# The first transfers of a two-layer encoder trunk, laid anew by k-tile

## The chip, the core and the metric

The kernel runs on one core of a Trainium2 chip. The time is device microseconds (us) of one execution on that core. A profiled execution leaves a page and a trace, from which all rows below are taken. Engines are named as the profile names them: PE multiplies matrices, PEld loads its stationary operands, DVE and ACT work elementwise, POOL does small scalar work, SP issues most transfers; q at the end of a name (SPq, ACTq) is the engine's instruction queue, where transfers are issued.

## The reference, cut to what matters

The input x has 256 tokens of 1024 columns. Two layers follow each other; each normalises, multiplies by one wide projection w_in, runs two attention branches, merges them, and goes through a gated feed-forward block and a per-layer embedding. Only the first instructions of the first layer are touched:

```python
u = rms_norm(h, g_mix_pre)                    # h = x, gain g of 1024 columns
(gq, gk, gv, gg, ra_f, ra_b, aq, ak, av, gate_a, gate_b) = jnp.split(u @ w_in, offsets, axis=-1)
```

The kernel multiplies first by 1056 columns of w_in, from column 3072 on: 32 of the two decay ranks (ra_f, ra_b) and 1024 of the attention's queries (aq). It cuts them in blocks of 288, 384 and 384 (`RQ`). The row factor of the norm is applied after the product, so that the product can start from x times the gain.

## The kernel before, in words

Every product is done in three passes to keep float32 precision: an operand is split in a high part (rounded to the matmul's format fp32r) and a low part, the rest; the passes are high by high, high by low, low by high. For weights ACT casts `wh` from the raw tile and DVE subtracts to get `wl`; for activations ACT makes `high` from the transposed x in PSUM times the gain, and DVE makes `rest` (`rest` is named `low` for weights).

Weights come in units of about 1 MB (`Stream`, lines 248 to 366), through two raw buffers. The first four units are rows 0 to 255, 256 to 511 and so on of those 1056 columns; a unit holds two k-tiles of 128 rows. `FIRST` (line 54) cuts the first unit's transfer into one for each k-tile. `load` (line 285) issues the next unit's transfer when a raw buffer is promised, and calls `between` after each piece.

The start is an order written out by hand. `on` (line 139) ties each instruction to the one before it on the same `line` (engine or transfers), so that their order is kept. `start()` (line 830) is a generator: it issues some work, yields a count of ticks, and goes on after so many calls of `tick()`, which the matmul loops make. Before: x's first 512 columns of tokens 0 to 127 go on SP and of tokens 128 to 255 on ACT, then the gain; then unit 0 in two pieces, unit 1 whole, and x's other columns. PE runs warm-up matmuls on constants (`WARM`: 6 of 128 columns, 6 of 512, and 3 more of 512 after the first transposes). `gains` turns the gain, `turn(hf, k)` transposes 128 columns of one token half, `high` and `rest` split the result.

`rq_first` (line 1034) multiplies unit 0 k-tile by k-tile for both token halves, six PSUM accumulators at once, 18 matmuls a k-tile; the units 1 to 3 go through `rq_step` (line 1026), one accumulator at a time. `STEPS_FIRST` gives the order of units. The third unit (unit 2) is split inside `start()` at its end, from unit 3 on by `fill`. The small weights of the decay (`up_weights`, line 730, six transfers at lines 737 and 738) are issued behind whatever stood last on the transfers' line when the layer loop begins (line 942). A scheduler then orders each engine's instructions by its own estimate of when they are ready, within those ties, for the whole program.

The transfers of a queue use eight completion semaphores in turn, so a ninth transfer waits until the first has landed.

## Time and profile before

| | us |
|---|---|
| median of 3 runs | 922.12 (921.61 to 922.44) |
| the profiled execution | 921.18 |
| its span, first to last instruction | 919.5 |
| PE busy in it | 909.8 |

The span leaves out 1.7 us of the execution's own time. The page lists busy time by engine, the span in 40 slices, the transfers, the chain of work that ended last and the costliest groups; the trace answers for a stretch (timeline, windows) or for one tile. In a timeline a row merges instructions of one kind: start, length from the first start to the last end, engine, line, operands, count, and in brackets the idle time before it and what ended it. Instructions that go through `on` all have line 142, `mm` has 105, `passes` has 121.

### The profile page before, as it was taken

What the parts mean: (1) busy time and instruction counts of PE and PEld (TensorE: products, weight loads), DVE (VectorE), ACT (ScalarE), POOL (GpSimd) and SP (SyncE); (2) the same over time, 40 slices, a digit from 0 to 9 for tenths busy, and PEclk for the clock granted to TensorE, in tenths of its full rate; (3) what the DMA queues carried; (4) which work ended last, traced back from release to release, by engine and by line L of the source; (5) the groups of instructions that cost most, each with busy time, mean ns of one, the idle gap of its engine ahead of it and who ended that gap; (6) DMA issues with size and microseconds to landing.
All of it is one profiled execution on the core that took longest, in us unless ns stands there. A gap on an engine that the chain in (4) does not pass through costs nothing.

```text
span 919.5 us, 12425 instructions
## 1 busy us (share of the span) xinstructions
PE 909.8 (99%) x4673; PEld 775.9 (84%) x4673; DVE 783.3 (85%) x1003; ACT 582.7 (63%) x970; POOL 91.7 (10%) x149
## 2 busy tenths in 40 slices
PE   9999999999999999999999999999999999999996
PEld 8998888888888888888899988888888788888885
DVE  7889989987669998999779789798875899989984
ACT  7678767564567565566676687765544766565663
POOL 4700221300100000000114002200001000000000
PEclk9999999999999999999999999999999999999999
DMA  8663445657395655657576424454673846555361
GB/s 291 205 189 133 138 138 189 212 184 244 109 301 186 210 191 201 228 166 262 190 232 220 148 92 140 136 208 159 211 247 110 279 160 211 222 175 216 138 229 46
DMA packets 88679, 173.44 MB, mean 189 GB/s; under 512 B 3422, under 2 KB 26470, under 8 KB 88108
## 3 DMA queue, kind: packets, MB, share of 16 engines
q1 hardware_dynamic: 88460, 172.40, 55.5%
q8 instruction: 36, 0.59, 0.3%
q10 hardware_dynamic: 160, 0.27, 0.1%
q14 instruction: 23, 0.19, 0.1%
HBM read 169.50 MB, written 3.15 MB: 188 GB/s over the span
## 4 chain that ended last, share of the span: by engine, by line
PE 91%; DVE 3%; ACT 2%; DMA 2%; issue 1%; POOL 1%; ACTq 0%; POOLq 0%; DVEq 0%; SPq 0%
PE acc_0ffnin L121 12%; PE acc_1ffnin L121 11%; PE acc_0gate L121 7%; PE acc_1gate L121 7%; PE acc_0ffnin L105 7%; PE acc_1ffnin L105 7%; PE acc_0gqk L121 2%; PE acc_0wout L121 2%; PE acc_1gqk L121 2%; PE acc_1ple L121 2%; PE acc_1gg L121 2%; PE acc_0v L121 2%; PE acc_0merge L121 2%; PE acc_1merge L121 2%; PE acc_0gg L121 2%; PE acc_0rq L121 2%
## 5 line engine op out<-in xcount | busy, mean ns | idle before, releaser
L105 PE MATMUL acc_0ffnin<-wh_0ffnin,big_0ffnin 128*128 128x512 f32 x176 | 57.0, 393 | 0.0
L105 PE MATMUL acc_1ffnin<-wh_1ffnin,big_1ffnin 128*128 128x512 f32 x176 | 56.8, 392 | 0.0
L133 ACT CAST wh_1ffnin<-raw_1ffnin 128x1024 fp32r<-128x1024 f32 x38 | 38.5, 1048 | 26.0 <-PE acc_1ffnin L121 7.8
L133 ACT CAST wh_0ffnin<-raw_0ffnin 128x1024 fp32r<-128x1024 f32 x38 | 38.3, 1048 | 24.9 <-DMA raw_0ffnin<-in_w_ffn_out_dram 7.6
L133 DVE TENSOR_TENSOR wl_1ffnin<-raw_1ffnin,wh_1ffnin 128x1024 fp32r<-128x1024 f32 x38 | 44.9, 1221 | 7.9 <-ACT wh_1ffnin L133 7.8
L133 DVE TENSOR_TENSOR wl_0ffnin<-raw_0ffnin,wh_0ffnin 128x1024 fp32r<-128x1024 f32 x38 | 44.7, 1221 | 7.8 <-ACT wh_0ffnin L133 7.8
L121 PE MATMUL acc_1ffnin<-wh_1ffnin,big_1wout 128*128 128x512 f32 x168 | 42.5, 393 | 0.0
L121 PE MATMUL acc_0ffnin<-wh_0ffnin,big_0wout 128*128 128x512 f32 x168 | 42.4, 393 | 0.0
L105 PEld LDWEIGHTS acc_0ffnin<-wh_0ffnin,big_0ffnin 128*128 128x128 f32 x176 | 33.0, 188 | 7.1 <-DVE big_0ffnin L133 0.4
L105 PEld LDWEIGHTS acc_1ffnin<-wh_1ffnin,big_1ffnin 128*128 128x128 f32 x176 | 33.0, 188 | 6.7
L133 DVE TENSOR_TENSOR wl_1ffnin<-lent_1ffnin,wh_1ffnin 128x1024 fp32r<-128x1024 f32 x30 | 35.8, 1219 | 1.8 <-ACT wh_1ffnin L133 1.8
L133 DVE TENSOR_TENSOR wl_0ffnin<-lent_0ffnin,wh_0ffnin 128x1024 fp32r<-128x1024 f32 x30 | 35.8, 1219 | 1.7 <-ACT wh_0ffnin L133 1.7
L121 PEld LDWEIGHTS acc_1ffnin<-wh_1ffnin,big_1wout 128*128 128x128 f32 x168 | 31.1, 188 | 6.2
L121 PEld LDWEIGHTS acc_0ffnin<-wh_0ffnin,big_0wout 128*128 128x128 f32 x168 | 31.1, 188 | 6.2
L133 ACT CAST wh_1ffnin<-lent_1ffnin 128x1024 fp32r<-128x1024 f32 x30 | 30.7, 1053 | 7.9 <-PE acc_1ffnin L105 3.9
L133 ACT CAST wh_0ffnin<-lent_0ffnin 128x1024 fp32r<-128x1024 f32 x30 | 30.7, 1053 | 6.9 <-PE acc_0ffnin L105 3.9
L105 PE MATMUL acc_0ffnin<-wl_0ffnin,big_0ffnin 128*128 128x512 f32 x88 | 34.3, 390 | 0.0
L105 PE MATMUL acc_1ffnin<-wl_1ffnin,big_1ffnin 128*128 128x512 f32 x88 | 34.3, 389 | 0.0
L133 DVE TENSOR_TENSOR wl_0gate<-raw_0gate,wh_0gate 128x1024 fp32r<-128x1024 f32 x20 | 24.0, 1247 | 6.8 <-ACT wh_0gate L133 6.7
L133 ACT CAST wh_0gate<-raw_0gate 128x1024 fp32r<-128x1024 f32 x20 | 20.0, 1049 | 13.9 <-DMA raw_0gate<-in_w_o_attn_dram 6.1
L133 DVE TENSOR_TENSOR wl_1gate<-raw_1gate,wh_1gate 128x1024 fp32r<-128x1024 f32 x20 | 23.6, 1220 | 5.4 <-ACT wh_1gate L133 5.4
L133 ACT CAST wh_1gate<-raw_1gate 128x1024 fp32r<-128x1024 f32 x20 | 20.0, 1051 | 11.6 <-DMA raw_1gate<-in_w_o_attn_dram 5.6
(705 smaller groups left out, 2701.9 us busy)
## 6 DMA issues: line engine op xcount, KB each, us to landing
raw_0ffnin<-in_w_ffn_out_dram SPq DMA_DIRECT2D x11, 1024.0 KB, 6.0
raw_1ffnin<-in_w_ffn_out_dram SPq DMA_DIRECT2D x11, 1024.0 KB, 5.6
lent_0ffnin<-in_w_ffn_in_dram SPq DMA_DIRECT2D x6, 1024.0 KB, 7.6
lent_1ffnin<-in_w_ffn_in_dram SPq DMA_DIRECT2D x6, 1024.0 KB, 7.1
raw_0v<-in_w_in_dram SPq DMA_DIRECT2D x4, 1024.0 KB, 5.0
raw_0gate<-in_w_o_gla_dram SPq DMA_DIRECT2D x4, 1024.0 KB, 5.1
raw_0gate<-in_w_o_attn_dram SPq DMA_DIRECT2D x4, 1024.0 KB, 5.2
raw_0wout<-in_w_ffn_in_dram SPq DMA_DIRECT2D x8, 512.0 KB, 6.4
```

The costliest lines, as they stand in the source:

```text
L105: return nc.tensor.matmul(o, lhsT, rhs, start=start, stop=stop)
L121: nc.tensor.matmul(o, x, y, start=start and n == 0, stop=stop and n == len(seq) - 1, **kw)
L133: return nc.scalar.copy(hi, src), nc.vector.tensor_tensor(out=lo, in0=src, in1=hi.bitcast(F32), op=ALU.subtract)
```

## The change

x is loaded in four transfers of all 256 tokens: columns 0 to 127 first, then 128 to 255, 256 to 511 and 512 to 1023, all on SP; the gain is the first transfer on ACT's queue. Of the weights the first transfer is 288 columns of k-tile 0, then its other 768, x's next columns, k-tile 1, x's next, k-tiles 2 and 3 apart, x's last. The warm-up on PE is 6 + 3 + 1 matmuls in place of 6 + 6 + 3. The first `high` of token half 1 is made by DVE. Unit 1 is also multiplied by `rq_first`, and transposes and splits are spread over the ticks of both units, so the transfers of `up_weights` are now tied behind x's last columns, and no longer behind the load of unit 2.

```diff
--- before.py
+++ after.py
@@ -49,9 +49,9 @@
 UNIT = 2112
 RQ = ((0, 288), (288, 672), (672, 1056))
 
-WARM = 6, 6, 3
-
-FIRST = (0, 0, 1056), (1, 0, 1056)
+WARM = 6, 3, 1
+
+FIRST = ((0, 0, 288), (0, 288, 1056), (1, 0, 1056)), ((0, 0, 1056), (1, 0, 1056))
 C_GQ, C_GK, C_GV, C_GG, C_RA = 0, 512, 1024, 2048, 3072
 C_AQ, C_AK, C_GA, C_GB = 3104, 4128, 4640, 5664
 
@@ -149,12 +149,10 @@
 
     grow = mid()[0:8, 0:P]
 
-    def load_x(hf, j, e="dma", q=nc.sync):
-        c = slice(j * 512, (j + 1) * 512)
-        on(e, q.dma_start, h[:, hf, c], a["x"][0, hf * P : (hf + 1) * P, c])
-
-    load_x(0, 0)
-    load_x(1, 0, "act", nc.scalar)
+    def load_x(c0, c1):
+        on("dma", nc.sync.dma_start, h[:, :, c0:c1], a["x"][0, :, c0:c1].rearrange("(s p) c -> p s c", p=P))
+
+    load_x(0, 128)
     on("act", nc.scalar.dma_start, grow, a["g_mix_pre"][0].rearrange("(k p) -> k p", p=P))
 
 
@@ -205,7 +203,7 @@
     plan = []
     for l in range(DEPTH):
         w = a["w_in"][l]
-        plan += [unit_rows(w, n, C_RA, C_RA + 1056, FIRST if l + n == 0 else None) for n in range(4)]
+        plan += [unit_rows(w, n, C_RA, C_RA + 1056, FIRST[n] if l == 0 and n < 2 else None) for n in range(4)]
         for c0 in (C_AK, C_GQ, C_GK, C_GV, C_GV + 512, C_GG, C_GG + 512):
             plan += [unit(w, kh, c0) for kh in range(2)]
         by_block = lambda w, c: [unit(w, kh, c + j * 512) for j in range(2) for kh in range(2)]
@@ -741,10 +739,11 @@
         return wup
 
 
+    x1 = [lambda: load_x(128, 256), lambda: None]
+    ws.load(lambda: x1 and x1.pop()())
+    load_x(256, 512)
     ws.load()
-    ws.load()
-    load_x(0, 1)
-    load_x(1, 1)
+    load_x(512, 1024)
     unit_a, unit_b = ws.pieces()
     warm = accp.tile([P, 512], F32, tag="acc", name="warm")
     gcol = small(8, "gcol", 1)
@@ -829,37 +828,45 @@
 
     def start():
         cut = lambda piece, c: [t[:, c] for t in piece]
+
+        def split_cut(piece):
+            for c in RQ:
+                on("act", nc.scalar.copy, *(t[:, slice(*c)] for t in piece[::2]))
+
         gains()
         for hf in range(2):
             turn(hf, 0)
-        for hf in range(2):
-            high(hf, 0)
         warm_up(WARM[2], True)
-        turn(0, 1)
-        turn(1, 1)
-        turn(0, 2, 3)
-        for c in RQ:
-            on("act", nc.scalar.copy, *(t[:, slice(*c)] for t in unit_a[::2]))
+        high(0, 0)
+        hi = uT.at(0, 1, P, P)[0][:, 0, :]
+        on("dve", nc.vector.tensor_scalar, out=hi, in0=banks[1, 0][:, 0:P], scalar1=gcol[:, 0:1], scalar2=None, op0=ALU.mult)
+        split_cut(unit_a)
         rest(0, 0)
         rest(1, 0)
         low(*cut(unit_a, slice(0, 288)))
-        high(0, 1)
-        high(1, 1)
         low(*cut(unit_a, slice(288, 1056)))
-        on("act", nc.scalar.copy, unit_b[0], unit_b[2])
+        yield 2
+        for hf in range(2):
+            turn(hf, 1)
+        for hf in range(2):
+            high(hf, 1)
+        split_cut(unit_b)
         rest(0, 1)
         rest(1, 1)
-        high(0, 2, 3)
-        low(*unit_b)
-        rest(0, 2, 3)
+        low(*cut(unit_b, slice(0, 288)))
+        low(*cut(unit_b, slice(288, 1056)))
         ws.load()
         unit_c, unit_d = ws.pieces()
-        yield 2
+        yield 3
+        turn(0, 2, 3)
+        high(0, 2, 3)
+        rest(0, 2, 3)
+        split_here(*unit_c)
+        yield 1
         turn(1, 2, 3)
         high(1, 2, 3)
         rest(1, 2, 3)
-        yield 4
-        split_here(*unit_c)
+        yield 2
         split_here(*unit_d)
         ws.load()
         for hf in range(2):
@@ -1031,16 +1038,16 @@
             passes(o[:, : c1 - c0], parts, u == 0, u == 3, u == 0)
             tick()
 
-        def rq_first(os_):
+        def rq_first(os_, u):
 
             for k in range(2):
                 for hf, ps in ((0, (0, 2)), (1, (0, 2)), (0, (1,)), (1, (1,))):
-                    ah, al = uT.tok(k, hf)
+                    ah, al = uT.tok(2 * u + k, hf)
                     for b, (c0, c1) in enumerate(RQ):
-                        h, lo = (t[:, k * 1056 + c0 : k * 1056 + c1] for t in us[0])
+                        h, lo = (t[:, k * 1056 + c0 : k * 1056 + c1] for t in us[u])
                         for p in ps:
                             x, y = ((ah, h), (ah, lo), (al, h))[p]
-                            mm(os_[hf, b][:, : c1 - c0], x, y, k + p == 0, False)
+                            mm(os_[hf, b][:, : c1 - c0], x, y, u + k + p == 0, False)
                     tick()
 
         steps = [(int(x[0]), b, int(x[1])) for x in (STEPS if l else STEPS_FIRST) for b in range(3)]
@@ -1050,10 +1057,10 @@
                 us.append(ws.take())
             if (hf, b) not in o:
                 o[hf, b] = acc()
-            if l + u:
+            if l or u > 1:
                 rq_step(o[hf, b], hf, b, u)
             elif (hf, b) == (1, 2):
-                rq_first(o)
+                rq_first(o, u)
             if all(s[2] != u for s in steps[n + 1 :]):
                 ws.done()
             if u == 3:
```

## The prediction

> **What bounds the kernel now.** I read the page first, then PE's timeline of the first 31 us, then those of ACT, DVE and SP there, the queue's waits, and the transfers' rate by stretches. The page:

> ```profile
> span 919.5 us, 12425 instructions
> PE 909.8 (99%) x4673; PEld 775.9 (84%) x4673; DVE 783.3 (85%) x1003; ACT 582.7 (63%) x970; POOL 91.7 (10%) x149
> ```

> PE idles 9.7 us in all. The chain of waits in order of time shows where: about 4.6 us ahead of its first useful work, the rest at the other end, so that from 4.61 on an earlier PE ends the kernel earlier, as long as nothing makes it wait:

> ```profile
> 1.22 3.25 DMA mid_start<-in_g_mix_pre_dram
> 4.61 0.73 PE aux_start L142 x3
> ...
> 14.77 16.64 PE acc_0rq L121 x102
> ```

> The change can only act in the ramp before 31 us. PE's timeline there (start, length, operation, count):

> ```profile
> 1.04 0.82 PE L105 MATMUL warm<-seed 128*128 128x128 bf16 x6 [1.04 <-POOL seed L142]
> 1.66 2.77 PE L105 MATMUL warm<-keep,seed 128*128 128x512 bf16 x6
> 4.61 0.24 PE L142 MATMUL aux_start<-ident,mid_start 8*128 8x8 f32 x1 [0.18 <-DMA mid_start<-in_g_mix_pre_dram]
> 4.78 0.55 PE L142 MATMUL aux_start<-ident,h 128*128 128x128 f32 x2
> 5.17 0.81 PE L105 MATMUL warm<-keep,seed 128*128 128x512 bf16 x3
> 5.82 0.67 PE L142 MATMUL aux_start<-ident,h 128*128 128x128 f32 x4
> 6.30 2.71 PE L105 MATMUL acc_0rq<-wh_start,big_start 128*128 128x288 f32 x12
> ...
> 10.03 2.10 PE L105 MATMUL acc_0rq<-wh_start,big_start 128*128 128x288 f32 x12
> ...
> 12.94 0.60 PE L142 MATMUL aux_start<-ident,h 128*128 128x128 f32 x4
> ...
> 19.62 0.69 PE L121 MATMUL acc_0rq<-wh_start,big_start 128*128 128x288 f32 x4
> ...
> 20.80 0.29 PE L121 MATMUL acc_0rq<-wl_start,big_start 128*128 128x288 f32 x1
> ```

> The reader is to see four marks: the gain's landing starts the transposes at 4.61, the first product starts at 6.30, k-tile 1 takes 10.03 to 12.94, and unit 2 starts at 19.62 and uses the low part of its second half at 20.80.

> **Step 1: the first data.** The row of x's tile and the windows of the transfers:

> ```profile
> DMA to landing us min/median/max: 3.3/3.5/7.9
> 1.80:2.30 0.50, 0.50 (x3) 0.17 (x2) 0.00 (x0) 0.45 (x1) 0.50 (x1) 1.00 0.99 61
> 2.30:3.80 1.50, 1.50 (x5) 0.46 (x3) 0.00 (x0) 0.83 (x1) 0.10 (x1) 1.00 1.00 374
> ```

> The last number is GB/s. Bytes flow from 2.3 on at 374. Before, 512 KB of x and the gain go first: 0.53 MB / 374 = 1.4 us, so to 3.7, and they land at 4.1 to 4.5. Now 132 KB go first: 0.36 us. That is 1.05 us less, so the transposes can start at 4.61 - 1.05 = 3.55. Narrow rows may move more slowly (bound: no gain, 4.61); the floor is the end of the warm-up on PE. Its spacing is (2.77 - 0.63) / 5 = 0.43, from the first row below, so three wide ones from 1.66 end at 2.95, and the six that were cut cost nothing, since PE would only have waited.

> ```profile
> L105 PE MATMUL warm<-keep,seed x9: 379/634/634, 1.7 to 5.6; 128*128 128x512 bf16 x9
> ...
> L142 PE MATMUL aux_start<-ident,h x12: 272/273/444, 4.8 to 13.3; 128*128 128x128 f32 x12
> ```

> From the first transpose to the first product before: 6.30 - 4.61 = 1.69, through ACT:

> ```profile
> 5.26 0.63 ACT L142 ACTIVATE big_start<-aux_start,gcol_start 128x128 fp32r<-128x128 f32 x2 [2.13 <-PE aux_start L142]
> 5.81 1.26 ACT L142 CAST wh_start<-raw_start 128x288 fp32r<-128x288 f32 x3
> ```

> One of the two 0.3 us activations goes to DVE, which was idle there. So 1.69 - 0.27 = 1.4, and the first product starts at about 4.9, between 4.6 (transposes at 3.2) and 6.3. I take 4.8, **1.5 us earlier**.

> **Step 2: work that is owed.** Before, six transposes of x were done by 6.30, now two. Four at (0.60 - 0.27) / 3 = 0.11 (row at 12.94; a transpose alone lasts 0.27) are **0.44 us** paid later. The three splits of k-tile 1 in place of one cost ACT 1.26 instead of some 1.05, off PE's path.

> **Step 3: feeding PE.** Before, k-tile 0 with two transposes took 10.03 - 6.30 = 3.73, the fed k-tile 1 2.91: 0.6 us lost on casts. Now the 768 other weight columns end 660 KB into the stream, 1.8 us after 2.3, and land with a tail like the gain's at 4.5 to 4.9; two casts later, at 5.8, the last third of k-tile 0 can start. Between 4.8 and 5.8 PE has a third to two thirds of its work. Then ACT must wait: k-tile 1's transposes stand behind the first 12 products on PE (0.4 for the rest of the first half's, and 2.91 / 3 for six of the other half: 7.2), its two activations and three casts follow one another for 0.63 + 1.26 = 1.9 us, the first of them overlapping, so k-tile 1's last block comes at 8.9 to 9.1, when PE wants it at about 8.6. The loss is 0.6 + 0.3 = 0.9 if PE keeps the written order, 0.1 if the scheduler fills with the other half's products. Against the 0.6 of before: **+0.3, or a gain of 0.5**; I take +0.2, since its estimate reordered the first products before too. PE alone: 1.5 - 0.44 - 0.2 = **about 0.9 us earlier** at unit 2 (0.7 to 1.6).

> **Step 4: unit 2, where the gain meets its limit.** SP's timeline and waits, then ACT and DVE:

> ```profile
> 10.16 0.38 SPq L142 DMA_DIRECT2D raw_start<-in_w_in_dram  x1
> 10.65 0.41 SPq L737 DMA_DIRECT2D mid_start<-in_w_alpha_up_dram  x1
> ...
> 15.87 0.39 SPq L711 DMA_DIRECT2D mid_start<-in_rope_cos_dram  x1
> ```

> ```profile
> SPq L711 <- DMA raw_start<-in_w_in_dram: 1.3, 1, 1.3
> SPq L373 <- DMA h<-in_x_dram: 0.6, 1, 0.6
> ```

> ```profile
> 15.87 2.05 ACT L142 CAST wh_start<-raw_start 128x1056 fp32r<-128x1056 f32 x2
> 17.43 2.42 DVE L142 TENSOR_TENSOR wl_start<-raw_start,wh_start 128x1056 fp32r<-128x1056 f32 x2
> 5.80:10.50 4.70, 4.69 (x29) 4.05 (x29) 3.90 (x9) 3.86 (x11) 0.00 (x0) 1.00 1.02 402
> ```

> Unit 2's load is issued at 10.16, when unit 0's raw buffer is free, and lands at 15.87 (the rope transfer, eight issues later, waits 1.3 us for it to end). Casts and subtractions end at 17.43 + 2.42 = 19.85; PE uses them at 20.80, a slack of 0.95.

> Now the six small transfers of the decay weights are tied behind x's last columns, so they reach SP ahead of unit 2's load. Counted in order that load is the 18th transfer (x, gain, two of weights, x, weights, x, two of weights, x, the GLA gain, six small), and with eight semaphores in turn it waits for the tenth, x's last 512 KB. All early bytes are the same 2.9 MB at 402 GB/s; the last landed before at about 11.2 (10.50 and the same 0.5 to 0.7 tail), so the load is issued at 11.2 to 11.4, **1.1 us later**. Behind it in SP's queue stand unit 3's load and the rope tables. Unit 3's split ends at 24.00 and PE uses its low part at 26.14, 2.1 us later; POOL wants the ropes at 22.84, 7 us after their issue:

> ```profile
> 21.57 2.43 DVE L133 TENSOR_TENSOR wl_start<-raw_start,wh_start 128x1056 fp32r<-128x1056 f32 x2 [0.47 <-ACT wh_start L133]
> ```

> ```profile
> 26.14 0.30 PE L121 MATMUL acc_0rq<-wl_start,big_start 128*128 128x288 f32 x1
> ```

> ```profile
> 22.84 1.76 POOL L717 TENSOR_TENSOR rope_start<-mid_start 128x256 f32<-128x256 f32 x1
> ```

> If it lands as long after as before (5.7), unit 2's low part is ready at 20.95, later than before's use: gain -0.15. With the shortest landing of the early weight loads, 5.2 (row below), 20.45: gain 0.35. An order that issues the load first would leave step 3's 0.9. I take the load late and the short landing, which is nearest to how an empty queue behaved, **0.3 us**. DVE and ACT leave no other room: from 10 to 18 us they are busy all but a few tenths:

> ```profile
> DMA to landing us min/median/max: 5.2/5.6/6.3
> ```

> ```profile
> 10.00:15.00 5.00, 5.00 (x37) 4.96 (x36) 4.58 (x10) 4.94 (x13) 0.09 (x1) 1.00 0.88 302
> 15.00:20.00 5.00, 5.00 (x32) 5.00 (x31) 4.97 (x16) 3.87 (x7) 4.56 (x8) 1.00 0.95 294
> ```

> **Step 5: PE's speed.** The warm-up's two groups show two speeds: 0.43 us for 512 columns from 1.66, (0.81 - 0.38) / 2 = 0.22 from 5.17. The granted clock (third number from the end in the windows) reads 1.00 in every stretch quoted, so it does not show this. PE worked from 1.04 to about 5.1, with one break of 0.2, before it doubled. Now the warm-up ends at 2.95, and there are gaps until about 5.8. If the double speed comes by 6.8, it costs nothing, since step 4 absorbs it; each us after 5.8 costs PE 0.5. I take no cost.

> [...]

> **The sum.** The profiled execution has 921.18; less 0.3 it is 920.9. It was 0.94 below the median of the runs shown, so on their scale 922.12 - 0.3 = **921.8**. What a measurement of this kernel can tell from no change is about 0.2%, 1.84 us.

> **Rivals.** *Double speed comes late.* The unbroken work has to start anew with the first product: 4.8 + 4.0 = 8.8, so PE loses (8.8 - 5.8) / 2 = 1.5 of its 0.9: 0.6 slower, **922.8**. If the sparse products up to then don't count and a second 4 us pass (12.8), PE loses 3.5, 2.6 net: **924.8**, slower. It decides from 7.0 on (gain below 0.3), and passes 0.2% from 11.3 on. For it: the gaps; against it: before had a gap too, 4.4 to 4.6.

> *Unit 2 is not late.* The scheduler puts the load ahead of the small transfers, or PE takes other products first. Then step 3 holds: 0.9 to 1.6, with the transposes at 3.2 up to 1.9: **920.9**, 920.2 at best. Against it: SP's wait for a landing is in the rows.

> *The first bytes come no sooner.* Rows of 512 bytes in place of 2 KB, and the first packets' slow half microsecond (61 GB/s), eat the 1.05 us; then 0.44 is lost and hidden in unit 2's slack: **922.3**.

> **Chances.** Forecast 0.52; unit 2 in time 0.18, half of it beyond 0.2% faster; late speed once 0.14, a fifth of it beyond 0.2% slower; twice 0.08; no sooner 0.04; the whole program planned otherwise behind 31 us 0.04, half each way. Faster 0.09 + 0.02 = 0.11; slower 0.08 + 0.03 + 0.02 = 0.13; same 0.76. The range takes in the filled ramp and one late change of speed: 920.2 to 923.8; the forecast's own is 921.2 to 922.3.

> **What would show it.** Step 1: the gain's transpose near 3.5, the first product near 4.8. Step 3: k-tile 1 near 8.5. Step 4: the fourth large weight load on SP after the small ones, near 11.3, its cast near 16.7, and a PE gap near 20. Step 5: the spacing of 384-column products 0.17 from the start. I am wrong if that spacing is 0.33 beyond 8 us, if unit 2's load is issued near 10, or if PE has a gap after 31 us that it had not.

## The result, and the profile after

The changed kernel takes 924.39 us (median of 8 runs, 923.57 to 925.92), the kernel before, run beside it, 921.9 (920.7 to 922.7). The ratio is 1.0031, 95% interval 1.0021 to 1.004: slower by 0.3%, outside the range that was predicted (920.2 to 923.8), and close to the 924.8 of the rival in which the double speed comes late twice over. The profiled execution has 924.51.

The two lines of the page that answer to those shown of before, after the change:

```profile
span 922.8 us, 12427 instructions
PE 912.0 (99%) x4668; PEld 777.8 (84%) x4668; DVE 785.2 (85%) x1005; ACT 582.9 (63%) x971; POOL 91.7 (10%) x149
```

The span is 3.3 us longer, and PE is busy 2.2 us longer with the same products of data and five warm-up products fewer. So most of the loss isn't waiting: PE does the same work more slowly somewhere. PE's timeline after (start, length, operation, count, and in brackets the idle time before it and what ended that):

```profile
1.66 1.49 PE L105 MATMUL warm<-keep,seed 128*128 128x512 bf16 x3
3.07 0.27 PE L142 MATMUL aux_start<-ident,mid_start 8*128 8x8 f32 x1
...
3.76 0.63 PE L105 MATMUL warm<-keep,seed 128*128 128x512 bf16 x1
4.71 0.85 PE L105 MATMUL acc_0rq<-wh_start,big_start 128*128 128x288 f32 x2 [0.32 <-ACT wh_start L142]
6.46 3.41 PE L105 MATMUL acc_0rq<-wh_start,big_start 128*128 128x384 f32 x10 [0.90 <-ACT wh_start L142]
...
12.80 1.57 PE L105 MATMUL acc_0rq<-wh_start,big_start 128*128 128x384 f32 x8
...
22.07 1.63 PE L121 MATMUL acc_0rq<-wh_start,big_start 128*128 128x288 f32 x9
24.18 0.40 PE L121 MATMUL acc_0rq<-wl_start,big_start 128*128 128x288 f32 x1 [0.48 <-DVE wl_start L142]
...
34.67 2.07 PE L121 MATMUL acc_0kv<-wh_start,big_start 128*128 128x512 f32 x8
```

and the mark in the timeline of before that answers to the last of these, the first products of the keys:

```profile
31.39 2.07 PE L121 MATMUL acc_0kv<-wh_start,big_start 128*128 128x512 f32 x8
```

Read the lengths against the counts. The ten products that start at 6.46 take 3.41, about 0.32 apart; the eight at 12.80 take 1.57, 0.17 apart. PE runs at half speed until about 12.3 us, and the trace's own record of the clock turns to full at 12.29. Before, the same record turns at 5.06, ahead of the first product. The first product does start 1.6 us earlier (4.71 against 6.30), but unit 2 starts at 22.07 against 19.62, and the keys at 34.67 against 31.39. That last difference, 3.28, is about the whole of the longer span: behind the keys it grows to 3.8 and shrinks again, and the spans end 3.3 apart.

Two breaks in PE's work stand in the rows, 0.32 us ahead of 4.71 and 0.90 ahead of 6.46. A third, at 24.18, is a wait for unit 2's low part.

### The profile page after: what moved, and what is told of

It reads as the page before. It is cut to its first block, busy times and chain, and to the rows that moved or that the text cites. A ratio compares the mean times of both kernels' runs of the same rounds, so it can differ in the third digit from the quotient of the medians.

```text
span 922.8 us, 12427 instructions
## 1 busy us (share of the span) xinstructions
PE 912.0 (99%) x4668; PEld 777.8 (84%) x4668; DVE 785.2 (85%) x1005; ACT 582.9 (63%) x971; POOL 91.7 (10%) x149
## 4 chain that ended last, share of the span: by engine, by line
PE 93%; DVE 2%; ACT 2%; DMA 1%; issue 1%; POOL 1%; SPq 0%; POOLq 0%; DVEq 0%; ACTq 0%
PE acc_0ffnin L121 12%; PE acc_1ffnin L121 11%; PE acc_0gate L121 7%; PE acc_1gate L121 7%; PE acc_0ffnin L105 7%; PE acc_1ffnin L105 7%; PE acc_1rq L121 3%; PE acc_0wout L121 2%; PE acc_1gqk L121 2%; PE acc_1ple L121 2%; PE acc_0ple L121 2%; PE acc_1gg L121 2%; PE acc_0v L121 2%; PE acc_1merge L121 2%; PE acc_0merge L121 2%; PE acc_0gqk L121 2%
## 5 line engine op out<-in xcount | busy, mean ns | idle before, releaser
L105 PE MATMUL acc_0ffnin<-wh_0ffnin,big_0ffnin 128*128 128x512 f32 x176 | 57.0, 393 | 0.0
L105 PE MATMUL acc_1ffnin<-wh_1ffnin,big_1ffnin 128*128 128x512 f32 x176 | 56.9, 392 | 0.0
L133 ACT CAST wh_1ffnin<-raw_1ffnin 128x1024 fp32r<-128x1024 f32 x38 | 38.5, 1049 | 27.2 <-DMA raw_1ffnin<-in_w_ffn_out_dram 8.8
L133 ACT CAST wh_0ffnin<-raw_0ffnin 128x1024 fp32r<-128x1024 f32 x38 | 38.4, 1047 | 23.9 <-PE acc_0ffnin L105 9.7
L133 DVE TENSOR_TENSOR wl_1ffnin<-raw_1ffnin,wh_1ffnin 128x1024 fp32r<-128x1024 f32 x38 | 45.0, 1220 | 8.1 <-ACT wh_1ffnin L133 8.0
L133 DVE TENSOR_TENSOR wl_0ffnin<-raw_0ffnin,wh_0ffnin 128x1024 fp32r<-128x1024 f32 x38 | 44.9, 1221 | 7.3 <-ACT wh_0ffnin L133 7.2
L121 PE MATMUL acc_1ffnin<-wh_1ffnin,big_1wout 128*128 128x512 f32 x168 | 42.5, 393 | 0.0
L121 PE MATMUL acc_0ffnin<-wh_0ffnin,big_0wout 128*128 128x512 f32 x168 | 42.4, 393 | 0.0
L105 PEld LDWEIGHTS acc_0ffnin<-wh_0ffnin,big_0ffnin 128*128 128x128 f32 x176 | 33.0, 188 | 7.1 <-DVE big_0ffnin L133 0.4
L105 PEld LDWEIGHTS acc_1ffnin<-wh_1ffnin,big_1ffnin 128*128 128x128 f32 x176 | 33.1, 188 | 6.7
L133 DVE TENSOR_TENSOR wl_1ffnin<-lent_1ffnin,wh_1ffnin 128x1024 fp32r<-128x1024 f32 x30 | 35.8, 1218 | 2.4 <-ACT wh_1ffnin L133 2.4
L133 DVE TENSOR_TENSOR wl_0ffnin<-lent_0ffnin,wh_0ffnin 128x1024 fp32r<-128x1024 f32 x30 | 35.8, 1219 | 1.7 <-ACT wh_0ffnin L133 1.7
L121 PEld LDWEIGHTS acc_1ffnin<-wh_1ffnin,big_1wout 128*128 128x128 f32 x168 | 31.1, 188 | 6.2
L121 PEld LDWEIGHTS acc_0ffnin<-wh_0ffnin,big_0wout 128*128 128x128 f32 x168 | 31.1, 188 | 6.2
L133 ACT CAST wh_1ffnin<-lent_1ffnin 128x1024 fp32r<-128x1024 f32 x30 | 30.7, 1052 | 8.8 <-PE acc_1ffnin L105 3.9
L133 ACT CAST wh_0ffnin<-lent_0ffnin 128x1024 fp32r<-128x1024 f32 x30 | 30.7, 1053 | 7.0 <-PE acc_0ffnin L105 3.9
L105 PE MATMUL acc_1ffnin<-wl_1ffnin,big_1ffnin 128*128 128x512 f32 x88 | 34.4, 391 | 0.0
L105 PE MATMUL acc_0ffnin<-wl_0ffnin,big_0ffnin 128*128 128x512 f32 x88 | 34.3, 390 | 0.0
L133 DVE TENSOR_TENSOR wl_0gate<-raw_0gate,wh_0gate 128x1024 fp32r<-128x1024 f32 x20 | 24.0, 1247 | 7.1 <-ACT wh_0gate L133 7.0
L133 ACT CAST wh_0gate<-raw_0gate 128x1024 fp32r<-128x1024 f32 x20 | 20.0, 1050 | 14.0 <-DMA raw_0gate<-in_w_o_attn_dram 6.1
L133 DVE TENSOR_TENSOR wl_1gate<-raw_1gate,wh_1gate 128x1024 fp32r<-128x1024 f32 x20 | 23.6, 1221 | 5.5 <-ACT wh_1gate L133 5.4
L133 ACT CAST wh_1gate<-raw_1gate 128x1024 fp32r<-128x1024 f32 x20 | 20.0, 1048 | 11.7 <-DMA raw_1gate<-in_w_o_attn_dram 5.7
```

The lines of the kernel that those rows point to most:

```text
L105: return nc.tensor.matmul(o, lhsT, rhs, start=start, stop=stop)
L121: nc.tensor.matmul(o, x, y, start=start and n == 0, stop=stop and n == len(seq) - 1, **kw)
L133: return nc.scalar.copy(hi, src), nc.vector.tensor_tensor(out=lo, in0=src, in1=hi.bitcast(F32), op=ALU.subtract)
```

## The experiments

The theory was that the shorter warm-up and the two breaks (0.32 and 0.90 us) put off the double speed of TensorE (PE), from 5.06 to 12.29, and that the change's other edits matter little. The rivals were that the new order of transfers and products costs the time by itself, and that unit 1's order by k-tile does.

**The old warm-up in the new layout.** The warm-up is as long as before, all else is as changed:

```
-    WARM = 6, 3, 1
+    WARM = 6, 6, 3
```

> The changed kernel with the warm-up of before (6, 6, 3 in place of 6, 3, 1), nothing else. Theory (PE runs at half rate until 12.3 us because the shorter warm-up leaves breaks): the spacing of 384-column products falls from 0.32 to 0.17 us from the first products on; the first product comes at about 6.0, later by the three wide warm-ups of 0.43, yet the time falls by 2 to 3 us, to about 921.5 to 922.5. Rival (the order of work and the late load of unit 2 cost the time): the time stays at 924 or more, and PE still has a gap near 22 us.

Measured: 922.43 us (921.67 to 923.16, 11 runs) beside 921.72 of the kernel before, ratio 1.0006 (0.9996 to 1.0015). PE has no break ahead of 8 us, the record of the clock turns at 6.83, and the first product comes at 5.97, since it stands behind the warm-up. PE still waits 0.45 us for unit 2's low part, at 22.04. Of the change's loss some seven tenths go with this one line (2.49 us to 0.71); the rest can't be told from no change by this interval.

**The short warm-up in the old layout.** The other half alone, the kernel before with the shorter warm-up:

```
-    WARM = 6, 6, 3
+    WARM = 6, 3, 1
```

> The kernel before with the warm-up of the change (6, 3, 1), nothing else; transfers and order of products as before. Theory: PE idles between the warm-up and the landing of the gain at 4.5 us, so the double speed comes late, after 9 us, the products of k-tiles 0 and 1 take 0.32 us for 384 columns, and the time rises by 1 to 3 us, to 923 to 925. Rival (the transfers and the order cost the time, not the warm-up): the time stays within 0.5 us of before.

Measured: 923.05 (921.83 to 923.98, 11 runs), ratio 1.0012 (1.0003 to 1.0021). In the old layout the gain lands too late for a short warm-up, and PE's timeline of this kernel shows the break and what follows it:

```profile
2.51 0.63 PE L105 MATMUL warm<-keep,seed 128*128 128x512 bf16 x1
4.25 0.24 PE L142 MATMUL aux_start<-ident,mid_start 8*128 8x8 f32 x1 [1.10 <-DMA mid_start<-in_g_mix_pre_dram]
...
6.34 3.19 PE L105 MATMUL acc_0rq<-wh_start,big_start 128*128 128x288 f32 x12
...
10.57 2.10 PE L105 MATMUL acc_0rq<-wh_start,big_start 128*128 128x288 f32 x12
```

The first twelve products take 3.19, the next twelve 2.10. The clock turned at 8.37, 4.1 us after the break at 4.25 ended. It was expected after 9 us. Without any change of the transfers the cut of the warm-up costs about 1.3 us (0.3 to 1.9 by the interval).

**The breaks filled.** The changed kernel with one more wide warm-up product, and two products of constants behind the first two products. They go into a bank whose own first product overwrites them, so the result is the same and PE has something to do until the next cast:

```
-    WARM = 6, 3, 1
+    WARM = 6, 3, 2
+    FILL = 2
 ...
+    if (u, k, hf, b, ps[0]) == (0, 0, 0, 1, 0):
+        for _ in range(FILL):
+            with tc.issue_after(last.ins):
+                last = mm(os_[hf, b], seed, keep, True, True)
 ...
```

> The changed kernel with three more products of constants, put where PE had nothing to do: one more wide warm-up ahead of the first product and two wide ones, into an accumulator that its first true product overwrites, behind the first two products. Theory: without the break of 0.9 us at 5.6 us the double speed comes at 5 to 9 us in place of 12.3, at no cost in start (first product within 0.1 us of 4.7); the time falls to 921 to 923. If it comes by 6.8 the forecast of the blind prediction is tested as it stands: 921.8 less or more 0.6. Rival: the time stays at 924.

Measured: 922.11 (921.03 to 923.26, 11 runs), ratio 1.0006 (0.9997 to 1.0015). PE's timeline of it:

```profile
4.53 0.85 PE L106 MATMUL acc_0rq<-wh_start,big_start 128*128 128x288 f32 x2
5.18 1.08 PE L106 MATMUL acc_0rq<-keep,seed 128*128 128x512 bf16 x2
6.59 2.00 PE L106 MATMUL acc_0rq<-wh_start,big_start 128*128 128x384 f32 x10 [0.33 <-ACT wh_start L143]
...
21.73 0.40 PE L122 MATMUL acc_0rq<-wl_start,big_start 128*128 128x288 f32 x1 [0.20 <-DVE wl_start L143]
```

The ten products that took 3.41 take 2.00 here. The clock turned at 6.33. Three products that compute nothing win back about 2 us (922.11 against 924.39). The wait ahead of unit 2's low part (21.73) is still there. This is the prediction with its condition met, the double speed by 6.8. The time is 0.4 us above the kernel before, not 0.3 below, which the interval doesn't settle; but the keys start at 32.23, 0.84 later than before, so the late clock was not the only miss.

**Unit 1 by blocks again.** Only unit 0 goes by k-tile, as before the change:

```
-            if l or u > 1:
+            if l or u > 0:
```

> The changed kernel with unit 1 multiplied again accumulator by accumulator, as before; transfers, warm-up and the rest as changed. Theory: this part is not what costs; the double speed still comes late, and the time stays within 1 us of the changed kernel's 924.4. Rival (multiplying unit 1 by k-tile is what hurts): the time falls by 2 us or more.

Measured: 923.97 (922.19 to 925.92, 11 runs), ratio 1.0023 (1.0014 to 1.0032): not to be told from the changed kernel by these intervals, so unit 1's order isn't the main cause. But its profiled execution, the 922.19, had the double speed at 4.72, with the same early breaks as the changed kernel. Up to that moment its instructions are those of the changed kernel, so the late moment (12.29 there) isn't fixed by the program.

**The changed kernel once more.** Unaltered, beside the three kernels that come next:

> The changed kernel once more, unaltered, beside the others of this call. Theory (the double speed of TensorE comes late, at a moment that differs between executions, because its work breaks off at 4.4 and 5.6 us): 924.0 to 924.6, the 384-column products again 0.32 us apart beyond 8 us in the profiled execution, unless that execution is one of the early ones. Rival (the late moment was one odd execution and the loss comes from the order of work alone): products 0.17 us apart from about 8 us or sooner, and the time still near 924.4.

Measured: 923.52 (922.91 to 925.31, 9 runs), beside 921.47, ratio 1.0026 (1.0016 to 1.0036). The median is a little under what was expected, and the profiled execution (923.01) is one of the early ones: the clock turned at 4.56. That makes it the execution that shows the layout without the late clock. Its timeline of PE:

```profile
5.96 2.00 PE L105 MATMUL acc_0rq<-wh_start,big_start 128*128 128x384 f32 x10 [0.90 <-ACT wh_start L142]
...
19.27 1.62 PE L121 MATMUL acc_0rq<-wh_start,big_start 128*128 128x288 f32 x9
21.33 0.40 PE L121 MATMUL acc_0rq<-wl_start,big_start 128*128 128x288 f32 x1 [0.43 <-DVE wl_start L142]
...
31.83 2.07 PE L121 MATMUL acc_0kv<-wh_start,big_start 128*128 128x512 f32 x8
```

Unit 2 starts 0.35 us earlier than before (19.27 against 19.62), which is all that is left of a first product 1.8 us earlier. Then it loses more than that: from unit 2 to the keys it takes 12.56, before 11.77. The place of that loss is the wait at 21.33; the timelines of ACT and DVE in the same execution show its cause:

```profile
17.17 1.07 ACT L737 CAST mid_0rq<-mid_start 81x1024 fp32r<-81x1024 f32 x1
18.10 2.08 ACT L142 CAST wh_start<-raw_start 128x1056 fp32r<-128x1056 f32 x2
```

```profile
18.27 1.22 DVE L129 TENSOR_TENSOR mid_0rq<-mid_start,mid_0rq 17x1024 fp32r<-17x1024 f32 x1 [0.28 <-ACT mid_0rq L737]
19.50 0.61 DVE L142 SCALAR_TENSOR_TENSOR big_start<-aux_start,gcol_start,big_start 128x128 fp32r<-128x128 f32 x2
20.02 2.42 DVE L142 TENSOR_TENSOR wl_start<-raw_start,wh_start 128x1056 fp32r<-128x1056 f32 x2
```

The copy and the subtraction of the decay weights, 1.07 and 1.22 us, go ahead of unit 2's split, as their small transfers now go ahead of unit 2's load. Before they stood behind it.

The early clock doesn't bring this execution to the time before: it has 923.01 against 921.18, 1.8 us more, of which 0.44 is there at the keys. Another 0.58 is a wait behind them that no other execution here has, a gap after 31 us as the prediction had named it for a sign:

```profile
56.49 0.51 PE L105 MATMUL aux_0at<-big_0kv,mid_0at 128*128 128x256 f32 x2 [0.58 <-ACT big_0kv L133]
```

The other 0.8 isn't accounted for.

**The decay weights behind unit 2's split.** The copy and the subtraction are written into the order by hand, behind unit 2's; their transfers stay where they are:

```
-        nc.scalar.copy(wup, up)
-        vsub(wup[64:81], up[64:81], wup[64:81].bitcast(F32))
+        if l:
 ... (the second layer keeps the two lines)
+        else:
+            def convert():
+                on("act", nc.scalar.copy, wup, up)
+                low(wup[64:81], wup[64:81], up[64:81])
 ...
+            later.append(convert)
 ...
         for piece in ws.pieces():
             split_here(*piece)
+        later.pop()()
```

> The changed kernel with the decay weights' copy (ScalarE) and subtraction (VectorE) behind unit 2's split instead of ahead of it. Theory (two separate losses: some 2 us of late double speed, 0.5 to 0.75 of unit 2's low part coming late): the low part of unit 2 is ready 1.2 us sooner; with the products as late as they are (unit 2 from about 22) its gap of 0.5 to 0.6 near 23.5 goes, 923.8. Rival (unit 2's gap costs nothing of the end, since the products behind it have slack): 924.4 as the changed kernel.

Measured: 923.1 (922.16 to 924.85, 11 runs), ratio 1.0019 (1.001 to 1.0028), 0.4 under the changed kernel beside it, which these two spreads can't tell from nothing; the rows show more. ACT and PE of its profiled execution, whose clock turned at 4.19:

```profile
17.35 2.06 ACT L142 CAST wh_start<-raw_start 128x1056 fp32r<-128x1056 f32 x2 [0.20 <-DMA raw_start<-in_w_in_dram]
19.31 1.04 ACT L142 CAST mid_0rq<-mid_start 81x1024 fp32r<-81x1024 f32 x1
```

```profile
30.80 2.07 PE L121 MATMUL acc_0kv<-wh_start,big_start 128*128 128x512 f32 x8
```

The wait in unit 2 is gone, and unit 2 to the keys takes 11.75 (from 19.05 to 30.80), as before. The keys start 0.59 earlier than before: that is what the new layout wins there in this one execution, with an early clock and this order. At 71 us only 0.14 of it is left. The execution still had 922.16, as the transposes at 234 us waited 1.09 for VectorE (line 1430), a wait that the executions of before and of the unaltered changed kernel quoted here don't have there; why isn't settled.

**Both together.** The fillers and the late decay weights:

> The early double speed (one more wide warm-up product and two products of constants behind the first two products, in a bank that its own first product overwrites) together with the late decay weights. Theory: 922.1 less the gap of 0.5 to 0.6 near 21.2 = 921.5, the start of the keys' products 0.5 earlier than the 32.2 of the kernel with the fillers alone; within 0.2% of the kernel before. Rival (the gap only moves to the second half of unit 2 or to unit 3, whose load is no earlier): 922.0 to 922.2.

Measured: 921.22 (920.76 to 922.35, 11 runs) beside 921.47, ratio 0.9998 (0.9989 to 1.0006). The time before is back, and no more than that can be told. It is 1.9 us under the kernel with the late decay weights alone, measured beside it, so the three products of constants show their worth a second time. The rival was partly right in the profiled execution (922.35, the slowest of the runs): its keys start at 32.19, where 31.7 was expected, since PE waits one unit further on, for a subtraction of unit 3 that took 1.81 where each of the two took 1.2 before. PE, and then DVE (the view ends at 24 and shows the first of the two subtractions):

```profile
5.99 2.44 PE L106 MATMUL acc_0rq<-wh_start,big_start 128*128 128x384 f32 x10
...
26.81 0.41 PE L122 MATMUL acc_0rq<-wl_start,big_start 128*128 128x288 f32 x1 [0.43 <-DVE wl_start L134]
```

```profile
23.65 1.81 DVE L134 TENSOR_TENSOR wl_start<-raw_start,wh_start 128x1056 fp32r<-128x1056 f32 x1 [0.32 <-ACT wh_start L134]
```

The first row also shows the clock turning in the middle of the ten products (7.13): 2.44, between the 2.00 and the 3.41 of the others.

**One break closed, one left.** The warm-up product of the fillers' kernel without the fillers:

```
-    WARM = 6, 3, 1
+    WARM = 6, 3, 2
```

> The changed kernel with one more wide warm-up product (6, 3, 2) and no fillers: the break in TensorE's work at 4.4 us is closed, that at 5.6 to 6.5 us is left. Theory (any break of some tenths inside the stretch before the double speed puts it off): late again, products 0.32 us apart beyond 8 us, 923.3 to 924.4. Rival (the number of warm-up products decides, and the 0.43 us of one wide product is what lacked): double speed near 6.4, 922.1 as with the fillers.

Measured: 923.59 (921.36 to 924.86, 12 runs), ratio 1.0018 (1.001 to 1.0027). Its PE:

```profile
4.53 0.85 PE L105 MATMUL acc_0rq<-wh_start,big_start 128*128 128x288 f32 x2
6.36 3.41 PE L105 MATMUL acc_0rq<-wh_start,big_start 128*128 128x384 f32 x10 [0.98 <-ACT wh_start L142]
...
11.57 0.59 PE L105 MATMUL acc_0rq<-wh_start,big_start 128*128 128x384 f32 x2
```

The second break alone is enough: half speed to 10.68. The runs spread over 3.5 us, those of the two filled kernels over 2.2 and 1.6. A moment that comes early in some executions and late in others would give that, but the 33 runs of the kernel before beside them spread over 2.6, so the spread alone shows little.

**Further executions, for the moment.** Two more of the changed kernel and two of the kernel before. The theory has the changed kernel's clock turn at 4.2 to 4.7 us, ahead of the first break, or at 9.9 to 13, behind the second; the rival, for which any moment is as likely, has it at 6 to 9 as well:

> One more profiled execution of the changed kernel, for the moment of the double speed alone. [...] Rival (any moment is as likely as any other): 6 to 9 us as well.

> As the look before: 4.2 to 4.7 or 9.9 to 13 us by the theory, and the start of the keys' products (31.8 in the early execution, 34.7 in the late one) moves with it by half the difference; 6 to 9 us by the rival.

> A profiled execution of the kernel before, whose TensorE works without a pause of a tenth from 1.04 us but for 0.18 us at 4.4. Theory: one moment between 4.4 and 8 us. Rival: 9 us or later here too, so that lateness isn't a matter of the breaks.

> As the other look at the kernel before: between 4.4 and 8 us by the theory, 9 us or later by the rival.

All executions with their breaks. "Worked from" is the start of the stretch without a pause of 0.3 us or more in which the clock turned; "full at" is from the trace's record of the clock.

| kernel | pauses ahead of 7 us | worked from | full at | between | keys from | time |
|---|---|---|---|---|---|---|
| before | 0.18 | 1.04 | 5.06 | 4.0 | 31.39 | 921.18 |
| before, two more | none; 0.17 | 1.05; 1.04 | 5.90; 5.48 | 4.9; 4.4 | 31.35; 31.38 | 921.17; 921.25 |
| before, short warm-up | 1.10 | 4.25 | 8.37 | 4.1 | 31.93 | 922.35 |
| changed | 0.32, 0.90 | 6.46 | 12.29 | 5.8 | 34.67 | 924.51 |
| changed, second execution | 0.57 | 5.96 | 12.09 | 6.1 | 34.28 | 924.46 |
| changed, third execution | 1.35 | 6.73 | 12.83 | 6.1 | 35.05 | 925.62 |
| changed, once more | 0.90, after the turn | 1.05 | 4.56 | 3.5 | 31.83 | 923.01 |
| unit 1 by blocks | 0.36, which ends at the turn; 0.77 | 1.04 | 4.72 | 3.7 | 32.57 | 922.19 |
| decay weights late | 0.17, 0.71 | 1.04 | 4.19 | 3.1 | 30.80 | 922.16 |
| one break closed | 0.98 | 6.36 | 10.68 | 4.3 | 34.11 | 924.11 |
| old warm-up | none | 1.04 | 6.83 | 5.8 | 32.55 | 923.16 |
| fillers | 0.33, at the turn | 1.04 | 6.33 | 5.3 | 32.23 | 922.91 |
| fillers, decay weights late | none | 1.04 | 7.13 | 6.1 | 32.19 | 922.35 |

In every row the clock turns 3.1 to 6.1 us after the start of a stretch of steady work. The two further executions of the changed kernel (12.09 and 12.83) lie in the theory's second range, but no run shows one length of work after which the turn comes, nor what sets it between 3.1 and 6.1. Where the work broke off behind the first two products, ahead of 6 us, the clock had turned before that break (4.19 to 4.72) or turned from 10.68 on, never between. Where it went on, the clock turned at 5.06 to 7.13, and at 8.37 in the kernel before with the short warm-up, whose break of 1.10 lies ahead of the first product. Nothing stands for the "any moment is as likely" rival: none of the seven executions with that break turned between 4.72 and 10.68. The "late in the kernel before too" rival falls. One expectation missed: the keys should move by half the difference of the moments, and between the early execution and the second one they moved 2.45 for 7.5 us.

## Why the prediction was wrong

**Step 5 failed: "I take no cost".** It had said that the double speed costs nothing if it comes by 6.8, and each us after 5.8 costs 0.5. It came at 12.29. Its price for each us was somewhat high. The second execution of the changed kernel, with the clock at 12.09, starts its 384-column products at the same 5.96 as the early one, with the clock at 4.56:

```profile
5.96 3.41 PE L105 MATMUL acc_0rq<-wh_start,big_start 128*128 128x384 f32 x10 [0.57 <-ACT wh_start L142]
...
21.72 1.63 PE L121 MATMUL acc_0rq<-wh_start,big_start 128*128 128x288 f32 x9
...
34.28 2.07 PE L121 MATMUL acc_0kv<-wh_start,big_start 128*128 128x512 f32 x8
```

Unit 2 starts at 21.72 and 19.27, so the lateness alone cost **2.45 us**, where half of 12.09 - 5.8 is 3.1. What was wrong was the odds. The gaps were written down in that step, and the rival "twice late" had the moment (12.8) and the time (924.8; its own terms give 924.7) nearly exactly, at a chance of 0.08. That its time fits is in part luck: its price was too high, it held nothing of the loss in step 4, and its 4.0 us for one pass came from a single execution of before, where the runs have 3.1 to 6.1. The argument against it, that before had a gap too (4.4 to 4.6), doesn't hold: a pause of 0.18 did no harm in before, but pauses of 0.57 to 1.35 did. The step also took the warm-up to end PE's work at 2.95; the transposes followed at 3.07 and PE worked on to 4.39, so that in the early executions the double speed came at 4.2 to 4.7, ahead of the break behind the first two products.

**Step 1 held in its sum.** The gain's transpose was forecast at 3.55 and came at 3.07, right behind the warm-up; the first product was forecast at 4.8 and came at 4.71, in most other executions at 4.53. The way between them was 1.64 us (1.45 in the others) where the step's two times leave 1.25, so two errors cancelled, which is luck. One reading ahead of it was off, without effect: of PE's 9.7 idle us only 1.2 lie ahead of 4.61 (1.04 and 0.18 in its own rows), since the warm-up counts as busy.

**Step 2** was not measured by itself. The four transposes are there, later.

**Step 3 was mis-sized.** It gave PE 0.9 us at unit 2. With an early clock it is 0.35 (19.27 against 19.62). It had the other 768 weight columns landing at 4.5 to 4.9; ACT's rows show when it could begin with them:

```profile
5.40 0.93 ACT L142 CAST wh_start<-raw_start 128x384 fp32r<-128x384 f32 x2 [0.92 <-DMA raw_start<-in_w_in_dram]
```

```profile
5.89 0.93 ACT L142 CAST wh_start<-raw_start 128x384 fp32r<-128x384 f32 x2 [1.24 <-DMA raw_start<-in_w_in_dram]
```

The first is the early execution, the second the profiled one of the result. The landing is at 5.4 to 5.9, so two thirds of k-tile 0 come 0.5 to 1 us later than the latest that was reckoned, and this is the second break itself. The step took 374 GB/s for the early bytes; between 2.30 and 3.80 the early execution moved 226 and the profiled one 183, with its transfer engines as busy as before (shares of 1.02 and 0.92, before 1.00). The narrow rows of the third rival may be the reason, though not for the first bytes; no run tried them alone. The step that told of it, "between 4.8 and 5.8 PE has a third to two thirds of its work", counted it as lost work, not as a lost clock.

**Step 4 had the load right and missed what goes in front of it.** In the early execution SP's timeline and its waits are as forecast (issue at 11.2 to 11.4, behind x's last columns):

```profile
11.22 0.40 SPq L142 DMA_DIRECT2D raw_start<-in_w_in_dram  x1
```

```profile
SPq L142 <- DMA h<-in_x_dram: 2.0, 1, 2.0
```

In the profiled execution of the result another wait ends last, that for the low part of k-tile 1, since PE was late, and the load is issued at 12.90. The cast was forecast at 16.7 and came at 18.10 in the early execution: ACT was busy with activations up to 17.17, and then comes the copy, since the small transfers are ahead on SP, and their copy and subtraction are ahead on ACT and DVE as well. The step followed the small transfers through SP's queue alone. Their work on ACT and DVE (1.07 and 1.22) is the missing term, and it made the PE gap that was named for "near 20" (20.95 by the longer landing) longer and later, at 21.33 with an early clock. From unit 2 to the keys the profiled execution lost 12.60 - 11.77 = **0.83**, and with the two behind unit 2's split that loss was gone (11.75). The early bytes are 3.2 MB, not the 2.9 of that step; its landing was read from rows and doesn't rest on it.

**The sum by what was measured.** At the keys' first product: -0.35 for the layout (from the early execution), +2.45 for the clock (from the second), +0.35 for the later landing in the profiled execution (its 384-column products start at 6.46, not 5.96), +0.83 for the decay weights, together +3.28 against the forecast -0.3. The terms are differences of the same rows, so their sum has to close; what bears them out is the experiments. The rivals "unit 2 is not late" and "the first bytes come no sooner" did not happen. In the execution with the early clock the keys were still 0.44 late and the whole 1.8 us over before, so nothing speaks for "faster" in this version.

## What to carry to other kernels

Judge a warm-up by whether TensorE works without a break until the double speed is there. Here the break that mattered was the one behind the first products, when the next data was late (0.57 to 1.35 us, with the double speed at 10.68 to 12.83 where it had not come before that break): fill such a break with work on constants (6.33 and 7.13 in the two kernels that did), or don't shorten the warm-up (6.83). When transfers change places, follow each one past its queue to the engines that convert its data, because here what landed first was also converted first (1.07 us on ACT and 1.22 on DVE, ahead of unit 2's split). A start-up change must be looked at in several executions, since one trace can show the lucky moment (4.56 in one of the changed kernel, 12.09 to 12.83 in the other three).
